# A hybrid encoder block on one Trainium2 core: decay exponents by 16 products of 128 rows, and the weighing moved off GpSimd

## The chip, the cores and the metric

The kernel runs on one core of one Trainium2 chip. Five engines work side by side, each through its own instructions in order: TensorE (PE in the profile), the vector engine (DVE), the scalar engine (ACT), GpSimd (POOL) and SyncE (SP), which here issues most of the DMAs. Matmuls write to PSUM, of which this kernel uses eight banks of 128 x 512 floats; DVE and ACT read them here, and POOL works on SBUF tiles alone. The metric is the device time of one execution in microseconds (us), the median of several runs.

## The reference

One layer with x of 256 tokens by 2048 features, all in float32. The part that the change touches is the state-space mixer: 16 heads of 64 channels in 2 groups, in two directions, over two chunks of 128 tokens.

```python
hn = rmsnorm(h, mix_norm_pre)
z, xbc, dt_raw, u = split(hn @ w_in)
xbc = silu(dwconv(xbc, conv_w, conv_b)); xs, B, C = split(xbc)
dt = softplus(dt_raw + dt_bias); a = -exp(a_log)
# in each direction, in each chunk of 128 tokens:
acum = cumsum(dt * a)
seg = acum[l] - acum[s];  decay = exp(where(s <= l, seg, -inf))
y_diag = einsum(C @ B.T, decay, xs * dt)
y_off = C @ (state of the chunk before, decayed)
y = y_fwd + y_bwd + xs * d_skip
y = rmsnorm_by_group(y * silu(z)) * norm_w
mix = concat([y, pool_mixer(u)]) @ w_out
h = h + rmsnorm(mix, mix_norm_post)
```

After it come a gated conv-MLP of width 5632 and a per-layer embedding with a gate, which the change doesn't touch.

## The kernel before

A product in float32 is made of three products in a rounded 32-bit format: each operand is split into a high part (a cast on ACT, line 150) and the rest (a subtraction on DVE, line 151). Weights come by DMA into three raw buffers, and the splits into five buffers each for high and low part, so the splits run up to five panels of 1024 columns ahead of PE.

The mixer's stage runs in this order on PE. First the columns of dt and u (tiles dtu). Then three slabs of xbc, each 512 channels: slab 2 (B and C; its conv output is bc), slab 0 (xa) and slab 1 (xb), both for xs. A slab is made by feature_major in four units of 48 matmuls, then times_rows (xr), conv (five taps: per 128 channels one ACT instruction, line 420, and four DVE instructions, line 426, 16 in all), a tanh on ACT (line 626) and a product on DVE (line 628). Then z, by token_major: eight pairs of panels with 24 matmuls each. Then the output projection (wo).

After each unit of a slab, and after each pair of z, the function aside runs the next entry of the list work. An entry is a list of jobs. The jobs are the small steps of the mixer:

- seg_prep(i), i from 0 to 7 (chunk t, quarter q of the heads): four POOL instructions multiply the step sizes (high and low part, dah and dal) by a mask, into a page ap.
- seg(i): four matmuls of 128 x 512 with the strict masks m_gt and m_lt sum these to the exponents of both directions, in one bank; ACT takes the exponential into E.
- decays: four small products and an exponential for the decay between chunks (dec).
- pool_mix and pool_map: the pooling mixer; pool_map's result leaves PSUM by ACT (cath) and DVE (catl).
- cb(g): C times B; DVE multiplies it by the masks (cbm).
- weigh(t, g): w = cbm (backward) x dt on POOL, then plus cbm (forward) x dt, eight DVE instructions, then E = E x w on DVE.
- xs_turn: transposes xs to token rows.
- far(t) and skip(t): xs x dec and xs x d_skip, both on POOL.
- mix(t, g): yo, the part from the other chunk, then yd, eight products of E with xs, added up in y.

All these jobs share two PSUM banks under the tag misc; the slabs and z use six others. Pages (13 of 128 x 2048) and mids (3 of 128 x 1024) are the SBUF buffers. The order of the instructions on each engine is not the order of the program text: a planner sorts them by the time at which they could run under a model of costs, the earlier text first among those that are ready. On the chip each engine then keeps that order, so an instruction that waits holds up all behind it on its engine. issue_after ties an instruction behind another one on the same engine.

Of the kernel before, what the change touches and what calls it, by code (L numbers as in the profile page):

```python
# [16 lines left out]
P = 128  # L17
# [4 lines left out]
H = 16  # L22
# [29 lines left out]
def build(nc, a, out):  # L52
# [5 lines left out]
    with tile.TileContext(nc) as tc, \  # L58
# [27 lines left out]
        def mm(o, lhsT, rhs, start, stop):  # L86
            nc.tensor.matmul(o, lhsT, rhs, start=start, stop=stop, skip_group_check=True)  # L87
# [24 lines left out]
        small = ep.tile([P, 80 + 512], F32, name="small")  # L112
# [18 lines left out]
        mask = small[:, 80:].rearrange("p (m f) -> p m f", m=4)  # L131
# [348 lines left out]
        with tc.issue_after(half[0]), tc.issue_after(half[1]):  # L480
            xs_ = [page(f"x{t}") for t in range(2)]
            for t in range(2):
                load(xs_[t], x[t * P:(t + 1) * P, :])
            rx = row_rstd("rx", xs_)
            m_gt, m_lt = (ep.tile([P, P], F32R, name=n) for n in ("m_gt", "m_lt"))
            nc.vector.tensor_copy(m_gt, mask[:, 2, :])
            nc.vector.tensor_copy(m_lt, mask[:, 3, :])
            aneg = ep.tile([P, 32], F32, name="aneg")
            nc.scalar.activation(aneg, alog, AF.Exp)
            nc.gpsimd.tensor_scalar(aneg, aneg, -1.0, None, op0=ALU.mult)  # L490

# [42 lines left out]
        dah = ep.tile([P, 2, 32], F32R, name="dah")  # L534
        dal = ep.tile([P, 2, 32], F32, name="dal")
        nc.vector.tensor_tensor(da, dt, aneg.unsqueeze(1).to_broadcast([P, 2, 32]), op=ALU.mult)
        nc.vector.tensor_copy(dah, da)
        nc.vector.tensor_sub(dal, da, dah.bitcast(F32))
# [13 lines left out]

        ee = [page(f"E{t}") for t in range(2)]
        steps = {}

        def seg_prep(i):
            t, q = divmod(i, 4)
            ap_ = page(f"ap{i}", F32R).rearrange("p (a h l) -> p a h l", a=4, h=4)
            for j in range(4):
                d, src = j // 2, (dah.bitcast(F32), dal)[j % 2]  # L560
                hs = slice(d * H + 4 * q, d * H + 4 * q + 4)
                nc.gpsimd.tensor_tensor(ap_[:, j], src[:, t, hs].unsqueeze(2).to_broadcast([P, 4, P]),
                                        mask[:, d, :].unsqueeze(1).to_broadcast([P, 4, P]), op=ALU.mult)
            steps[i] = ap_

        def seg(i):
            t, q = divmod(i, 4)
            sps, ap_ = misc(f"seg{i}"), steps.pop(i)
            for j in range(4):
                mm(sps, (m_gt, m_lt)[j // 2], ap_[:, j].rearrange("p h l -> p (h l)"), j == 0, j == 3)  # L570
            nc.scalar.activation(ee[t][:, q * 512:(q + 1) * 512], sps, AF.Exp)
# [59 lines left out]
        def weigh(t, g):  # L631

            w = mid(f"w{t}{g}")
            nc.gpsimd.tensor_tensor(w.rearrange("p (h l) -> p h l", h=8),
                                    cbm[:, 1, g, t, :].unsqueeze(1).to_broadcast([P, 8, P]),
                                    dt[:, t, H + 8 * g:H + 8 * g + 8].unsqueeze(2).to_broadcast([P, 8, P]),
                                    op=ALU.mult)
# [10 lines left out]
        def far(t):  # L648
            xd[t] = page(f"xd{t}")[:, :1024]
            nc.gpsimd.tensor_tensor(by_head(xd[t]), by_head(xs[:, t * 1024:(t + 1) * 1024]),  # L650
                                    dec[:, t, :].unsqueeze(2).to_broadcast([P, H, 64]), op=ALU.mult)
# [5 lines left out]
        def mix(t, g):  # L657
# [3 lines left out]
            mm(po, cbm[:, 2, g, s, :], xd[s][:, g * 512:(g + 1) * 512], True, True)  # L661
# [10 lines left out]
        def job(f, *args):  # L672
            return lambda: f(*args)
# [3 lines left out]
            [job(seg_prep, 0)],  # L677
            [job(seg_prep, 1), job(pool_mix, 0), job(pool_mix, 1)],
            [job(seg_prep, 2), job(pool_mix, 2), job(pool_mix, 3), job(decays)],
            [job(seg_prep, 3), job(seg, 0)],  # L680
# [3 lines left out]
            [job(seg_prep, 4), job(seg, 1), job(pool_map, 0), job(pool_map, 1)],  # L684
            [job(seg_prep, 5), job(seg, 2), job(cb, bc, 0), job(cb, bc, 1)],
            [job(seg_prep, 6), job(seg, 3), job(pool_map, 2), job(pool_map, 3)],
            [job(seg_prep, 7), job(seg, 4), job(weigh, 0, 0)],
# [3 lines left out]
            [job(seg, 5), job(weigh, 0, 1)],  # L691
            [job(seg, 6), job(xs_turn, xa, 0)],
            [job(seg, 7), job(weigh, 1, 0)],
            [job(weigh, 1, 1)],
# [8 lines left out]
            [],  # L703
            [job(xs_turn, xb, 1)],
# [305 lines left out]
def laid_out(a):  # L1010

    def cols(*vs):
# [11 lines left out]
            masks().transpose(1, 0, 2).reshape(P, 4 * P)], axis=1),  # L1024
# [3 lines left out]
def masks():  # L1028
    j = np.arange(P)[:, None]
    l = np.arange(P)[None, :]  # L1030
    return np.stack([j <= l, j >= l, j > l, j < l]).astype(np.float32)

# [19 lines left out]
```

## Time and profile before

| | us |
|---|---|
| median of 3 runs | 1133.08 |
| lowest and highest | 1132.37, 1133.37 |
| the profiled execution | 1134.26 |
| its span in the trace | 1132.4 |

The mixer's stage in the profiled execution, by stretches of PE's work (busy us of each engine, and TensorE's granted clock as a share of full speed):

| stretch, us | what PE works on | PE | DVE | ACT | POOL | clock |
|---|---|---|---|---|---|---|
| 53 to 82 | slab 2 | 28.36 | 21.24 | 11.51 | 17.07 | 1.00 |
| 82 to 125.3 | slab 0 | 38.36 | 36.24 | 18.23 | 26.05 | 0.92 |
| 125.3 to 152.7 | slab 1 | 26.93 | 25.61 | 13.98 | 6.74 | 1.00 |
| 152.7 to 209 | z | 56.10 | 43.66 | 23.94 | 16.21 | 1.00 |

How to read it: a row of the timeline gives the start, the length, the engine, the line, the output and inputs and, in brackets, how long the engine was idle before and what ended that. Matmuls overlap in the pipeline, so one lasts longer than the distance from its start to the next start; the distance is its cost. All matmuls are recorded under line 87, the helper mm, so they are told apart by the tile they write.

### The profile page before, as it was taken

What the parts mean: (1) busy time and instruction counts of PE and PEld (TensorE: products, weight loads), DVE (VectorE), ACT (ScalarE), POOL (GpSimd) and SP (SyncE); (2) the same over time, 40 slices, a digit from 0 to 9 for tenths busy, and PEclk for the clock granted to TensorE, in tenths of its full rate; (3) what the DMA queues carried; (4) which work ended last, traced back from release to release, by engine and by line L of the source; (5) the groups of instructions that cost most, each with busy time, mean ns of one, the idle gap of its engine ahead of it and who ended that gap; (6) DMA issues with size and microseconds to landing.
All of it is one profiled execution on the core that took longest, in us unless ns stands there. A gap on an engine that the chain in (4) does not pass through costs nothing.

```text
span 1132.4 us, 15774 instructions
## 1 busy us (share of the span) xinstructions
PE 1114.5 (98%) x5979; PEld 960.3 (85%) x5979; DVE 937.4 (83%) x1266; ACT 637.2 (56%) x868; POOL 127.3 (11%) x124
## 2 busy tenths in 40 slices
PE   9998999999999999999999999999999999999996
PEld 9997988888888888888888888888888888887875
DVE  6579797699888877878778778888899999889796
ACT  6533543465674554545545445445677777786672
POOL 0274504300101100000000000000000000001001
PEclk9998999999999999999999999999999999999998
DMA  9952347555789999998999998996969688995673
GB/s 360 344 179 81 113 128 261 205 163 184 241 302 330 328 329 312 315 295 301 348 328 313 296 316 289 330 316 213 318 194 329 222 291 304 376 306 190 231 235 109
DMA packets 145995, 300.85 MB, mean 266 GB/s; under 512 B 5504, under 2 KB 98560, under 8 KB 137856
## 3 DMA queue, kind: packets, MB, share of 16 engines
q1 hardware_dynamic: 145360, 298.44, 77.5%
q0 software_dynamic: 272, 1.05, 0.5%
q8 instruction: 47, 0.77, 0.3%
q10 hardware_dynamic: 288, 0.36, 0.1%
q14 instruction: 28, 0.23, 0.1%
HBM read 268.37 MB, written 31.46 MB: 265 GB/s over the span
## 4 chain that ended last, share of the span: by engine, by line
PE 88%; DVE 6%; DMA 2%; ACT 2%; issue 1%; POOL 1%; SPq 0%; DVEq 0%; POOLq 0%; ACTq 0%
PE va L87 22%; PE ga L87 21%; PE dna L87 12%; PE woa L87 7%; PE gt L87 5%; PE z L87 4%; PE dtu L87 4%; PE xbc L87 3%; PE dns L87 2%; DVE cv L426 2%; PE dn0s L87 1%; DMA dn138t<-dns 1%; PE dn1s L87 1%; PE ple L87 1%; DMA dtur<-w_in 1%
## 5 line engine op out<-in xcount | busy, mean ns | idle before, releaser
L87 PE MATMUL ga<-wox,ug_0h 128*128 128x512 f32 x352 | 125.6, 395 | 0.0
L87 PE MATMUL ga<-wox,ug_1h 128*128 128x512 f32 x352 | 125.1, 394 | 0.0
L87 PE MATMUL va<-wox,uv_1h 128*128 128x512 f32 x352 | 124.8, 393 | 0.0
L87 PE MATMUL va<-wox,uv_0h 128*128 128x512 f32 x352 | 124.8, 393 | 0.0
L87 PE MATMUL ga<-wox,ug_1l 128*128 128x256 f32 x352 | 99.1, 282 | 0.0
L87 PE MATMUL ga<-wox,ug_0l 128*128 128x256 f32 x352 | 99.1, 282 | 0.0
L87 PE MATMUL va<-wox,uv_1l 128*128 128x256 f32 x352 | 99.1, 281 | 0.0
L87 PE MATMUL va<-wox,uv_0l 128*128 128x256 f32 x352 | 99.1, 281 | 0.0
L87 PEld LDWEIGHTS va<-wox,uv_1h 128*128 128x128 f32 x352 | 66.1, 188 | 15.0
L87 PEld LDWEIGHTS va<-wox,uv_0h 128*128 128x128 f32 x352 | 66.1, 188 | 15.0
L87 PEld LDWEIGHTS ga<-wox,ug_0h 128*128 128x128 f32 x352 | 66.1, 188 | 14.9
L87 PEld LDWEIGHTS ga<-wox,ug_1h 128*128 128x128 f32 x352 | 66.1, 188 | 14.9
L865 POOL TENSOR_TENSOR fc<-fc,rfb 128x1024 f32<-128x1024 f32 x11 | 28.0, 2547 | 438.6 <-ACT fc L864 438.6
L87 PEld LDWEIGHTS ga<-wox,ug_0l 128*128 128x128 f32 x352 | 66.2, 188 | 0.1
L87 PEld LDWEIGHTS va<-wox,uv_1l 128*128 128x128 f32 x352 | 66.2, 188 | 0.0
L87 PEld LDWEIGHTS ga<-wox,ug_1l 128*128 128x128 f32 x352 | 66.2, 188 | 0.0
L87 PEld LDWEIGHTS va<-wox,uv_0l 128*128 128x128 f32 x352 | 66.2, 188 | 0.0
L87 PE MATMUL dna<-dn_0h,hs 128*128 128x512 f32 x160 | 50.2, 394 | 0.2 <-DVE hs L884 0.2
L87 PE MATMUL dna<-dn_1h,hs 128*128 128x512 f32 x160 | 49.9, 393 | 0.0
L233 DVE TENSOR_TENSOR dnb<-dnb 128x1024 f32<-128x1024 f32 x24 | 30.3, 1261 | 13.6 <-DMA dnb<-w_ffn_down 13.5
L883 ACT CAST hs<-hid 128x512 fp32r<-128x512 f32 x44 | 27.1, 617 | 22.9 <-PE dna L87 18.3
L884 DVE TENSOR_TENSOR hs<-hid,hs 128x512 fp32r<-128x512 f32 x44 | 30.2, 687 | 9.7 <-ACT hs L883 9.7
(1898 smaller groups left out, 3148.3 us busy)
## 6 DMA issues: line engine op xcount, KB each, us to landing
dnb<-w_ffn_down SPq DMA_DIRECT2D x24, 1024.0 KB, 10.2
dns<-dnb SPq DMA_DIRECT2D x22, 1024.0 KB, 7.6
dn0r<-w_ffn_down SPq DMA_DIRECT2D x10, 1024.0 KB, 6.3
dn1r<-w_ffn_down SPq DMA_DIRECT2D x10, 1024.0 KB, 7.0
zr<-w_in SPq DMA_DIRECT2D x8, 1024.0 KB, 5.1
dtur<-w_in SPq DMA_DIRECT2D x14, 528.0 KB, 8.9
wo0r<-w_out SPq DMA_DIRECT2D x7, 1024.0 KB, 5.8
wo1r<-w_out SPq DMA_DIRECT2D x6, 1024.0 KB, 5.5
```

The source lines that it names most:

```text
L87: nc.tensor.matmul(o, lhsT, rhs, start=start, stop=stop, skip_group_check=True)
L233: nc.vector.tensor_add(v[:, 0:2], v[:, 0:2], v[:, 1::2])
L426: nc.vector.scalar_tensor_tensor(o[:, lo:hi], i[:, lo + d:hi + d], vec(wcol + j * wstep + f), o[:, lo:hi], op0=ALU.mult, op1=ALU.add)
L865: nc.gpsimd.tensor_tensor(cv.rearrange("p (f t) -> p f t", f=4), cv.rearrange("p (f t) -> p f t", f=4), rfb.unsqueeze(1).to_broadcast([P, ...
L883: nc.scalar.copy(t[:, :512], src)
L884: nc.vector.tensor_sub(t[:, 512:], src, t[:, :512].bitcast(F32))
```

## The change

The exponents. Instead of sums over 128 tokens for each seg, seg_sums takes the running sums once for all: four products (cps, 64 rows by 128 columns for each of four pairs of chunk and direction), their high part (seg_h) and the rest (seg_c). Eight ACT instructions spread them into two pages: seg_x (the moving side) and seg_w (the weights), whose other rows hold selectors of heads, filled ahead of the first slab; the rows from 64 on are zero. seg(i) is then two products of 128 rows by 512 columns, one for each direction, in two banks: ACT copies the first to E, DVE takes the minimum of E and the second, ACT the exponential. The masks m_gt and m_lt and the whole of seg_prep are gone.

The weighing. The first half of weigh goes from one POOL instruction to eight ACT instructions; far goes from POOL to DVE. The jobs are placed anew in work: the segs from slab 2's last unit to slab 1's second, weigh(0, 0) in slab 0, weigh(0, 1) in slab 1, weigh(1, 0) and weigh(1, 1) in z's third and fourth pair. yo is tied behind the last matmul that stands before it in the text, for mix(0, 0) the last of z's sixth pair.

```diff
         def mm(o, lhsT, rhs, start, stop):
-            nc.tensor.matmul(o, lhsT, rhs, start=start, stop=stop, skip_group_check=True)
+            last["pe"] = ins(nc.tensor.matmul(o, lhsT, rhs, start=start, stop=stop, skip_group_check=True))
...
+        low, among, four = small[:64, 592:593], small[:64, 593:597], small[:64, 597:601]
...
-            m_gt, m_lt = (ep.tile([P, P], F32R, name=n) for n in ("m_gt", "m_lt"))
-            nc.vector.tensor_copy(m_gt, mask[:, 2, :])
-            nc.vector.tensor_copy(m_lt, mask[:, 3, :])
+            seg_w = page("seg_w", F32R)
+            nc.scalar.activation(seg_w[64:], xs_[0][64:], AF.Copy, scale=0.0)
+            seg_w = seg_w.rearrange("p (a q s) -> p a q s", a=4, q=4)
+            seg_x = page("seg_x", F32R)
+            nc.scalar.activation(seg_x[64:], xs_[0][64:], AF.Copy, scale=0.0)
+            seg_x = seg_x.rearrange("p (a i l) -> p a i l", a=4, i=4)
+            for a_ in range(4):
+                nc.scalar.activation(seg_w[:32, a_], four[:32].unsqueeze(2).to_broadcast([32, 4, P]), AF.Copy,
+                                     scale=-1.0)
+                nc.scalar.copy(seg_x[32:64, a_], among[32:].unsqueeze(2).to_broadcast([32, 4, P]))
...
-        dah = ep.tile([P, 2, 32], F32R, name="dah")
-        dal = ep.tile([P, 2, 32], F32, name="dal")
+        da4 = ep.tile([P, 2, 2, 4, H], F32, name="da4")
         nc.vector.tensor_tensor(da, dt, aneg.unsqueeze(1).to_broadcast([P, 2, 32]), op=ALU.mult)
-        nc.vector.tensor_copy(dah, da)
-        nc.vector.tensor_sub(dal, da, dah.bitcast(F32))
+        for d in range(2):
+            nc.vector.tensor_scalar(da4[:, :, d], da[:, :, d * H:(d + 1) * H].unsqueeze(2).to_broadcast([P, 2, 4, H]),
+                                    1.0 - 2.0 * d, None, op0=ALU.mult)
...
-        def seg_prep(i):
-            t, q = divmod(i, 4)
-            ap_ = page(f"ap{i}", F32R).rearrange("p (a h l) -> p a h l", a=4, h=4)
-            for j in range(4):
-                d, src = j // 2, (dah.bitcast(F32), dal)[j % 2]
-                hs = slice(d * H + 4 * q, d * H + 4 * q + 4)
-                nc.gpsimd.tensor_tensor(ap_[:, j], src[:, t, hs].unsqueeze(2).to_broadcast([P, 4, P]),
-                                        mask[:, d, :].unsqueeze(1).to_broadcast([P, 4, P]), op=ALU.mult)
-            steps[i] = ap_
+        def seg_sums():
+            cps = misc("cps")
+            for a_ in range(4):
+                mm(cps[:64, a_ * P:(a_ + 1) * P], da4[:, a_ // 2, a_ % 2].rearrange("p r h -> p (r h)"),
+                   mask[:, 3 * (a_ % 2), :], True, True)
+            hi, c = page("seg_h", F32R)[:64, :512], page("seg_c")[:64, :512]
+            nc.scalar.copy(hi, cps[:64, :])
+            nc.vector.scalar_tensor_tensor(c, hi.bitcast(F32), low, cps[:64, :], op0=ALU.mult, op1=ALU.add)
+            c4 = c.rearrange("p (a l) -> p a l", a=4)
+            for i in range(4):
+                nc.scalar.activation(seg_x[:32, :, i, :], c4[:32], AF.Copy, scale=among[:32, i:i + 1])
+                nc.scalar.activation(seg_w[32:64, :, i, :], c4[32:], AF.Copy, scale=four[32:, i:i + 1])
 
         def seg(i):
             t, q = divmod(i, 4)
-            sps, ap_ = misc(f"seg{i}"), steps.pop(i)
-            for j in range(4):
-                mm(sps, (m_gt, m_lt)[j // 2], ap_[:, j].rearrange("p h l -> p (h l)"), j == 0, j == 3)
-            nc.scalar.activation(ee[t][:, q * 512:(q + 1) * 512], sps, AF.Exp)
+            ps = [misc(f"seg{i}{d}") for d in range(2)]
+            for d in range(2):
+                mm(ps[d], seg_w[:, 2 * t + d, q], seg_x[:, 2 * t + d].rearrange("p i l -> p (i l)"), True, True)
+            e = ee[t][:, q * 512:(q + 1) * 512]
+            nc.scalar.copy(e, ps[0])
+            nc.vector.tensor_tensor(e, ps[1], e, op=ALU.min)
+            nc.scalar.activation(e, e, AF.Exp)
...
             w = mid(f"w{t}{g}")
-            nc.gpsimd.tensor_tensor(w.rearrange("p (h l) -> p h l", h=8),
-                                    cbm[:, 1, g, t, :].unsqueeze(1).to_broadcast([P, 8, P]),
-                                    dt[:, t, H + 8 * g:H + 8 * g + 8].unsqueeze(2).to_broadcast([P, 8, P]),
-                                    op=ALU.mult)
+            for h in range(8):
+                nc.scalar.activation(w[:, h * P:(h + 1) * P], cbm[:, 1, g, t, :], AF.Identity,
+                                     scale=dt[:, t, H + 8 * g + h:H + 8 * g + h + 1])
...
         def far(t):
             xd[t] = page(f"xd{t}")[:, :1024]
-            nc.gpsimd.tensor_tensor(by_head(xd[t]), by_head(xs[:, t * 1024:(t + 1) * 1024]),
+            nc.vector.tensor_tensor(by_head(xd[t]), by_head(xs[:, t * 1024:(t + 1) * 1024]),
                                     dec[:, t, :].unsqueeze(2).to_broadcast([P, H, 64]), op=ALU.mult)
...
-            mm(po, cbm[:, 2, g, s, :], xd[s][:, g * 512:(g + 1) * 512], True, True)
+            with tc.issue_after(last["pe"]):
+                mm(po, cbm[:, 2, g, s, :], xd[s][:, g * 512:(g + 1) * 512], True, True)
...
         work.extend([
-            [job(seg_prep, 0)],
-            [job(seg_prep, 1), job(pool_mix, 0), job(pool_mix, 1)],
-            [job(seg_prep, 2), job(pool_mix, 2), job(pool_mix, 3), job(decays)],
-            [job(seg_prep, 3), job(seg, 0)],
+            [],
+            [job(pool_mix, 0), job(pool_mix, 1)],
+            [job(pool_mix, 2), job(pool_mix, 3), job(decays), job(seg_sums)],
+            [job(seg, 0), job(seg, 1)],
         ])
         bc = xbc(2)
         work.extend([
-            [job(seg_prep, 4), job(seg, 1), job(pool_map, 0), job(pool_map, 1)],
-            [job(seg_prep, 5), job(seg, 2), job(cb, bc, 0), job(cb, bc, 1)],
-            [job(seg_prep, 6), job(seg, 3), job(pool_map, 2), job(pool_map, 3)],
-            [job(seg_prep, 7), job(seg, 4), job(weigh, 0, 0)],
+            [job(seg, 2), job(pool_map, 0), job(pool_map, 1)],
+            [job(cb, bc, 0), job(cb, bc, 1), job(seg, 3)],
+            [job(seg, 4), job(weigh, 0, 0), job(pool_map, 2)],
+            [job(seg, 5), job(pool_map, 3)],
         ])
         xa = xbc(0)
         work.extend([
-            [job(seg, 5), job(weigh, 0, 1)],
-            [job(seg, 6), job(xs_turn, xa, 0)],
-            [job(seg, 7), job(weigh, 1, 0)],
-            [job(weigh, 1, 1)],
+            [job(seg, 6)],
+            [job(seg, 7), job(weigh, 0, 1)],
+            [job(xs_turn, xa, 0)],
+            [],
         ])
...
             [],
             [],
-            [],
-            [job(xs_turn, xb, 1)],
+            [job(weigh, 1, 0)],
+            [job(xs_turn, xb, 1), job(weigh, 1, 1)],
             [job(far, 1), job(skip, 0), job(far, 0), job(skip, 1)],
             [job(mix, 0, 0)],
```

The nine further columns of small (low, among and four) come with the constants, by a new function head_rows:

```python
def head_rows():
    p = np.arange(P)[:, None]
    i = np.arange(4)[None, :]
    return np.concatenate([-((p // 16) % 2), p % 4 == i, -1.0 * (p % 16 // 4 == i)], axis=1).astype(np.float32)
```

More of the change, by code (lines that the diff above doesn't have):

```diff
@@ L111, in build @@
         vt = cp.tile([P, V_N - V_SCW], F32, name="vt")
-        small = ep.tile([P, 80 + 512], F32, name="small")
+        small = ep.tile([P, 89 + 512], F32, name="small")
         last, sums_ = {}, {}
@@ L130, in build @@
         dtb, alog, dsk = small[:, :32], small[:, 32:64], small[:, 64:80]
-        mask = small[:, 80:].rearrange("p (m f) -> p m f", m=4)
+        mask = small[:, 80:592].rearrange("p (m f) -> p m f", m=4)
+        low, among, four = small[:64, 592:593], small[:64, 593:597], small[:64, 597:601]
         def vec(i):
@@ L553, in build @@
         ee = [page(f"E{t}") for t in range(2)]
-        steps = {}
-        def seg_prep(i):
-            t, q = divmod(i, 4)
-            ap_ = page(f"ap{i}", F32R).rearrange("p (a h l) -> p a h l", a=4, h=4)
-            for j in range(4):
-                d, src = j // 2, (dah.bitcast(F32), dal)[j % 2]
-                hs = slice(d * H + 4 * q, d * H + 4 * q + 4)
-                nc.gpsimd.tensor_tensor(ap_[:, j], src[:, t, hs].unsqueeze(2).to_broadcast([P, 4, P]),
-                                        mask[:, d, :].unsqueeze(1).to_broadcast([P, 4, P]), op=ALU.mult)
-            steps[i] = ap_
+        def seg_sums():
[10 more added lines that the diff above has]
+                nc.scalar.activation(seg_w[32:64, :, i, :], c4[32:], AF.Copy, scale=four[32:, i:i + 1])
         def seg(i):
             t, q = divmod(i, 4)
-            sps, ap_ = misc(f"seg{i}"), steps.pop(i)
-            for j in range(4):
-                mm(sps, (m_gt, m_lt)[j // 2], ap_[:, j].rearrange("p h l -> p (h l)"), j == 0, j == 3)
-            nc.scalar.activation(ee[t][:, q * 512:(q + 1) * 512], sps, AF.Exp)
+            ps = [misc(f"seg{i}{d}") for d in range(2)]
[5 more added lines that the diff above has]
+            nc.scalar.activation(e, e, AF.Exp)
         cat = Panel.__new__(Panel)
@@ L1023, in laid_out @@
                             (P, 80)),
-            masks().transpose(1, 0, 2).reshape(P, 4 * P)], axis=1),
+            masks().transpose(1, 0, 2).reshape(P, 4 * P), head_rows()], axis=1),
     }
```

## The prediction

> **What bounds the kernel now.** I read the page first, for the engine that is busy most and for the chain of work that ended last.
>
> ```profile
> PE 1114.5 (98%) x5979; PEld 960.3 (85%) x5979; DVE 937.4 (83%) x1266; ACT 637.2 (56%) x868; POOL 127.3 (11%) x124
> PE 88%; DVE 6%; DMA 2%; ACT 2%; issue 1%; POOL 1%; SPq 0%; DVEq 0%; POOLq 0%; ACTq 0%
> ```
>
> PE is busy for 98% of the span. So a gain is either PE work that disappears, or one of PE's few waits. These come from the view of PE's waits, whole span:
>
> ```profile
> PE seg L87 <- DVE catl L189: 4.9, 1, 4.9
> PE dps L87 <- DVE mixt L585: 0.6, 1, 0.6
> PE xbc L87 <- DVE xb_0l L151: 0.5, 1, 0.5
> ```
>
> All three lie in the stretch that the change edits. The largest is in PE's timeline (start, length, idle before). The rows ahead of it give two prices: a pair of pool_maps takes 92.16 - 88.89 = 3.27 us, and a unit of 48 xbc matmuls 5.7, from 92.16 to 97.92:
>
> ```profile
> 88.89 3.62 PE L87 MATMUL pw<-mixt,poolw 128*128 128x256 f32 x16
> 92.16 0.47 PE L87 MATMUL xbc<-hnh,xb_0h 128*128 128x256 f32 x1
> ...
> 97.92 0.28 PE L87 MATMUL xbc<-hnh,xb_1l 128*128 128x256 f32 x1
> 103.14 1.19 PE L87 MATMUL seg<-ap,m_gt 128*128 128x512 f32 x2 [4.94 <-DVE catl L189]
> ```
>
> and the stretches after it (length, PE busy, PEld, DVE, ACT, POOL, granted clock, DMA) say what the wait costs beyond itself:
>
> ```profile
> 103.10:109.00 5.90, 5.86 (x16) 4.79 (x17) 3.50 (x7) 2.52 (x4) 1.36 (x1) 0.52 0.57 192
> 109.00:110.00 1.00, 1.00 (x11) 1.00 (x10) 0.99 (x6) 0.56 (x2) 0.53 (x1) 1.00 0.34 129
> ```
>
> After the wait the granted clock averages 0.52 for 5.9 us, then is full again: 5.9 x 0.48 = 2.83 us of work lost. What makes catl late is DVE's conv in front of it. DVE's timeline, and the durations of line 426 in the first and the second conv (min/median/max):
>
> ```profile
> 83.93 14.24 DVE L426 SCALAR_TENSOR_TENSOR cv<-xr,vt,cv 128x254 f32<-128x254 f32 x16
> 126.80 6.39 DVE L426 SCALAR_TENSOR_TENSOR cv<-xr,vt,cv 128x254 f32<-128x254 f32 x16
> L426 DVE SCALAR_TENSOR_TENSOR cv<-xr,vt,cv x16: 472/1255/1257, 83.9 to 97.7; 128x254 f32<-128x254 f32 x8, 128x255 f32<-128x255 f32 x8
> L426 DVE SCALAR_TENSOR_TENSOR cv<-xr,vt,cv x16: 470/472/474, 126.8 to 132.7; 128x254 f32<-128x254 f32 x8, 128x255 f32<-128x255 f32 x8
> ```
>
> The same 16 instructions take 14.24 us in one slab and 6.39 in the next. What differs is POOL (the stretch of the first conv, fifth busy time, and a group from 53 to 210 us):
>
> ```profile
> 84.00:97.00 13.00, 13.00 (x95) 12.41 (x94) 13.00 (x15) 3.58 (x5) 12.30 (x12) 1.00 0.12 44
> L562 POOL TENSOR_TENSOR ap<-dal,small 128x512 fp32r<-128x512 f32 x16 | 22.4, 1400 | 0.0
> ```
>
> POOL is busy for 12.30 of 13.00 us, with seg_prep, and DVE's instruction takes 1255 ns; in the second conv, in the pause after seg_prep, it takes 472.
>
> **What the change removes.** *The decay matmuls.* Each seg now has two 512-column products instead of four:
>
> ```profile
> 81.34 0.62 PE L87 MATMUL seg<-ap,m_gt 128*128 128x512 f32 x2
> 81.80 0.62 PE L87 MATMUL seg<-ap,m_lt 128*128 128x512 f32 x2
> 71.97 2.02 PE L87 MATMUL mx<-pmat,u 128*128 128x136 f32 x16
> 73.74 0.37 PE L87 MATMUL xbc<-hnh,xb_0h 128*128 128x256 f32 x1
> ```
>
> Two start 0.46 after the other two, so a product is 0.23 us and 16 fewer save 3.68. PE also gains four fp32 products of 128 columns (cps). The mx group is two pool_mix jobs, 8 fp32 products, in 16 records of 136 columns; they take 73.74 - 71.97 = 1.77; the new ones are 8 records, so 0.88. Bounds: 0.4 if half of that overlaps, 1.1 if PE must wait for a weight load.
>
> *seg_prep on POOL* goes altogether. The first conv then takes 6.39 instead of 14.24, 7.85 us less in front of th, cv and catl. Nothing on DVE then is late for PE: the wait of 4.94 and its 2.83 go, and with the contention the two small waits (0.6 for a mixt copy behind a stretched split, 0.5 for a split), together 1.1.
>
> **What it adds.** The prices:
>
> ```profile
> 202.06 0.69 DVE L670 TENSOR_TENSOR y<-y,yd 128x512 f32<-128x512 f32 x1 [1.56 <-PE yd L87]
> L639 DVE SCALAR_TENSOR_TENSOR w<-cbm,dt,w 128x128 f32<-128x128 f32 x32 | 12.1, 444 | 1.8 <-POOL w L634 1.8
> L643 DVE TENSOR_TENSOR E<-E,w 128x1024 f32<-128x1024 f32 x3 | 3.6, 1215 | 0.0
> L409 DVE TENSOR_TENSOR xr<-xbc,rxb 128x512 f32<-128x512 f32 x3 | 2.0, 678 | 0.0
> L189 DVE SCALAR_TENSOR_TENSOR catl<-pw,vt,cath 128x256 fp32r<-128x256 f32 x8 | 3.7, 480 | 1.5 <-ACT cath L188 1.3
> L571 ACT ACTIVATE E<-seg 128x512 f32<-128x512 f32 x8 | 4.7, 593 | 0.5 <-PE seg L87 0.5
> L420 ACT ACTIVATE cv<-xr,vt 128x256 f32<-128x256 f32 x8 | 4.4, 593 | 0.0
> L611 ACT ACTIVATE cbm<-cb 128x128 f32<-128x128 f32 x4 | 1.1, 278 | 3.4 <-DVE cbm L609 3.3
> 82.00:125.30 43.30, 38.36 (x250) 35.65 (x249) 36.24 (x53) 18.23 (x30) 26.05 (x22) 0.92 0.29 98
> 125.30:152.70 27.40, 26.93 (x213) 25.92 (x212) 25.61 (x50) 13.98 (x19) 6.74 (x4) 1.00 0.31 100
> ```
>
> Each seg gets an ACT copy (0.59) and a DVE min (0.69, same form as y plus yd) before its exp: 4.7 us on ACT, 5.5 on DVE in all. weigh's POOL pass becomes eight ACT instructions, each between 0.28 (128 wide, from PSUM) and 0.59 (256 wide, two vectors); I take 0.35, 2.8 per call, as the width is that of the cheaper row. Does this fit? In the two slabs DVE was busy 36.24 + 25.61 = 61.85. Minus 7.85 (conv), minus the two of four weighs that move into z (2 x (12.1/4 + 1.2) = 8.5), plus 5.5: 51. PE's own time there is 70.7 - 8.2 (stall and clock) - 3.2 (segs 1 to 7) = 59. ACT: 18.23 + 13.98 + 4.7 + 5.6, 42 of 59. Neither sets the pace.
>
> ACT's one-time work for seg_w and seg_x (two clears 2048 wide, eight copies 512 wide) lies before the first slab:
>
> ```profile
> 36.34 1.92 ACT L391 ACTIVATE rxj<-x 128x2048 f32<-128x2048 f32 x1
> 40.00:60.00 20.00, 20.00 (x143) 20.00 (x142) 11.71 (x22) 10.60 (x15) 2.64 (x5) 1.00 0.84 288
> 51.65 0.56 ACT L514 ACTIVATE u<-dtu,rx0r 128x352 f32<-128x352 f32 x1 [6.52 <-PE dtu L87]
> ```
>
> 2 x 1.92 + 8 x 0.59 = 8.6 us, against 6.52 idle just before L514 and 9.4 from 40 to 60 (ACT busy 10.60): covered. If only the 6.52 served, 2.1 would fall on u's evacuation, which frees banks for the first slab: bounds 0 to 2.1, taken 0. seg_sums' chain (hi copy, c, eight more 512-wide ACT copies, about 6 us) runs under unit 3 of slab 2, 48 matmuls or 5.7 us, and the splits are several panels ahead: taken 0, up to 1.
>
> far on DVE (two ops of 1024, 1.2 each as the E product) and the late weighs sit under z. The tie moves nothing; the chain of waits already has yo behind six pairs (96 + 48 matmuls, 24 to a pair):
>
> ```profile
> 152.89 22.26 PE z L87 x96
> 176.02 11.10 PE z L87 x48
> 187.12 0.86 PE yo L87 x2
> ```
>
> *The new wait.* A seg takes both misc banks and gives the second back only after the min, which in slab 0's first unit is queued on DVE behind the conv. PE's arrival at pool_map 1, counted from the start of slab 0: segs 0 and 1, 48 matmuls, seg 2, pool_map 0 (half of 3.27) = 0.9 + 5.7 + 0.5 + 1.6 = 8.7. DVE, from the same point: last matmul's length 0.3 + xr 1.36 + two mins 1.38 + conv 6.39 + min 0.69 = 10.1. So 1.4 us if the matmuls stay in the order of the job list, 0 if others are put between, as the transposes show (xt, xbc, xt):
>
> ```profile
> 138.56 0.60 PE L617 MATMUL xt<-ident,cv 128*128 128x128 f32 x4
> 138.92 0.36 PE L87 MATMUL xbc<-hnh,xb_0h 128*128 128x256 f32 x1
> ...
> 139.41 0.65 PE L617 MATMUL xt<-ident,cv 128*128 128x128 f32 x4
> ```
>
> I take 0.7. Behind it wait catl, then cb; but th, its product (1.2 each, as the E product) and four catl (0.48 each) end by 10.1 + 2.4 + 1.9 = 14.4 on DVE, and PE comes to cb at 8.7 + 1.6 + 5.7 = 16.
>
> **Sum.** 3.68 - 0.88 + 4.94 + 2.83 + 1.1 - 0.7 = 10.97 us. The profiled execution took 1134.26 (span 1132.4), so 1123.3 in its terms; it stands 1.18 above the median of the runs, so 1133.08 - 10.97 = **1122.1**.
>
> **Rivals.** *One long wait stays.* If two splits (1024 wide, 1.2 each as the E product) are put ahead of the conv on DVE, PE's 1.4 us becomes 3.8, and as after the 4.94 the clock may drop, 2.8 more. 11.67 (the sum without its 0.7) less 6.6 leaves 5.1: 1128. For it: the catl wait had just this shape. Against: in the second slab the conv ran at 6.39 and PE waited 0.5.
>
> *Every hand-over of the two banks is unfilled* (slower). Then PE idles for copy and min, 0.59 + 0.69 = 1.28, at each of eight segs: 10.3, leaving 1.4 of gain. It decides from the first drop of the clock (2.8), which turns this to a loss of 1.4; with two drops the loss is 4.3, 1137.4. Against: the xt rows show such gaps filled, and the idles of 0.6 and 0.5 cost only themselves. [...]
>
> *The contention stays (the change doesn't do what it says).* If the first conv is slow for another reason, stall and clock loss stay and the mins add to it: 3.68 - 0.88 - 1.4 = 1.4, 1131.7. The 1255 against 472 ns speaks against it.
>
> **How the numbers follow.** A change under 0.2% (2.3 us) can't be told from none. The forecast has 0.75, with its own range 1119.8 (no new wait 1121.4, cps at its lower bound 0.5 less, a run's scatter) to 1125; one long wait 0.12; contention 0.03; the slower rival 0.08; 0.02 is left for a loss I don't see. Faster 0.75 + 0.12 = 0.87, same 0.03, slower 0.10. The range goes to 1130.5 to hold the 1128 case with its scatter.
>
> **What would show it.** Right: the first conv near 6.4 us; no PE idle over 2 us between 53 and 200; clock 1.00 in every stretch there; seg steps 0.46; z beginning near 141 instead of 152.7. Wrong: PE idle at a seg or pool_map with a min (or seg_x) as releaser; a clock of 0.50; the first conv still near 14; ACT late at 51 us. The forecast fails if the waits on the two banks add up to more than 4 us.

## The result, and the profile after

The median is 1123.84 us (four runs, 1123.31 to 1123.89) against 1132.94 for the kernel before (four runs, 1132.37 to 1133.37): a ratio of 0.9918, interval 0.9907 to 0.9930, a gain of 9.1 us. The profiled execution after took 1123.86 us (span 1122.1), so it stands at its median, where the one before, 1134.26, stood 1.2 above.

From the page of the changed kernel, the busy times and the chain of work that ended last:

```profile
PE 1109.2 (99%) x5971; PEld 957.8 (85%) x5971; DVE 925.4 (82%) x1275; ACT 664.3 (59%) x927; POOL 76.0 (7%) x86
PE 95%; ACT 2%; DVE 1%; issue 1%; POOL 1%; DMA 0%; POOLq 0%; DVEq 0%; ACTq 0%
```

PE's share of the chain rose from 88 to 95%, DVE's fell from 6 to 1. POOL lost 51 us of work and ACT gained 27. The view of PE's waits, from 50 to 200 us, where the first line was 4.9 before, has one line above 0.2:

```profile
PE seg L87 <- ACT seg_x L579: 0.7, 1, 0.7
```

Busy time by stretch (length, PE, PEld, DVE, ACT, POOL, granted clock, DMA share, GB/s):

```profile
82.00:115.00 33.00, 32.28 (x231) 30.37 (x230) 27.48 (x54) 26.26 (x47) 0.00 (x0) 1.00 0.37 115
115.00:140.00 25.00, 24.99 (x198) 24.33 (x197) 23.59 (x42) 17.40 (x30) 0.00 (x0) 1.00 0.44 151
140.00:200.00 60.00, 59.80 (x303) 49.13 (x302) 45.84 (x67) 29.89 (x48) 16.87 (x10) 1.00 0.60 209
```

The clock is full in all three, and POOL has nothing left in the two slabs. The first conv, in DVE's timeline, cut in two by a min:

```profile
87.64 1.77 DVE L428 SCALAR_TENSOR_TENSOR cv<-xr,vt,cv 128x254 f32<-128x254 f32 x4
89.33 0.69 DVE L589 TENSOR_TENSOR E<-seg,E 128x512 f32<-128x512 f32 x1
89.93 4.82 DVE L428 SCALAR_TENSOR_TENSOR cv<-xr,vt,cv 128x255 f32<-128x255 f32 x12
94.66 0.69 DVE L589 TENSOR_TENSOR E<-seg,E 128x512 f32<-128x512 f32 x1
```

It takes 1.77 + 4.82 = 6.59 us instead of 14.24. PE's timeline has the one wait left in this stretch, a seg of the third slab made (slab 1), and the beginning of z:

```profile
85.68 0.73 PE L87 MATMUL seg<-seg_x,seg_w 128*128 128x512 f32 x2 [0.69 <-ACT seg_x L579]
...
130.37 0.63 PE L87 MATMUL seg<-seg_x,seg_w 128*128 128x512 f32 x2
130.83 0.28 PE L87 MATMUL xbc<-hnh,xb_0h 128*128 128x256 f32 x1
...
143.10 0.63 PE L87 MATMUL z<-z_0h,hnh 128*128 128x512 f32 x2
```

A seg is 130.83 - 130.37 = 0.46 us for PE, half of before, and z begins at 143.10 instead of 152.72.

### The profile page after: what moved, and what is told of

It is laid out like the page before. It is cut to its first block, busy times and chain, and to the rows that moved or that the text cites. A ratio compares the mean times of both kernels' runs of the same rounds, so it can differ in the third digit from the quotient of the medians.

```text
span 1122.1 us, 15775 instructions
## 1 busy us (share of the span) xinstructions
PE 1109.2 (99%) x5971; PEld 957.8 (85%) x5971; DVE 925.4 (82%) x1275; ACT 664.3 (59%) x927; POOL 76.0 (7%) x86
## 4 chain that ended last, share of the span: by engine, by line
PE 95%; ACT 2%; DVE 1%; issue 1%; POOL 1%; DMA 0%; POOLq 0%; DVEq 0%; ACTq 0%
PE va L87 22%; PE ga L87 21%; PE dna L87 14%; PE woa L87 7%; PE xbc L87 6%; PE gt L87 5%; PE dtu L87 4%; PE z L87 4%; PE dns L87 3%; PE dn0s L87 1%; PE dn1s L87 1%; PE ple L87 1%; PE pw L87 1%; PE yd L87 0%; PE gts L87 0%
```

## The experiments

Ratios are against the kernel before, timed beside each on the same chip. "After" means the changed kernel. Whole times also hold what differs at the beginning and the end of an execution, so the table gives, for each profiled execution, the time, the start of PE's first matmul of slab 2, and what PE takes from there to its first matmul of z, the stretch that the change edits (all in us, from the traces).

| kernel | profiled execution | slab 2 begins | slab 2 to z |
|---|---|---|---|
| before | 1134.26 | 52.91 | 99.81 |
| before, profiled again | 1132.27 | 52.93 | 98.54 |
| before, weigh and far moved alone | 1131.98 | 52.54 | 98.69 |
| before, seg_prep once | 1124.81 | 52.75 | 91.26 |
| after | 1123.86 | 53.39 | 89.71 |
| after, POOL work put back | 1135.15 | 52.81 | 100.80 |
| after, weigh and far back on POOL | 1123.88 | 52.54 | 89.69 |
| after, weighs at their old places | 1131.26 | 54.57 | 89.83 |
| after, yo untied | 1123.06 | 52.56 | 89.73 |
| after, seg products twice | 1126.68 | 52.83 | 93.10 |
| after, 64 rows | 1126.00 | 52.69 | 92.44 |
| after, spreads on POOL | 1123.14 | 52.77 | 89.52 |
| after, spreads on POOL, maps in pairs | 1123.10 | 52.80 | 89.39 |

Slab 2 begins from 0.9 us earlier to 1.2 later in the kernels made from after than in after itself, though nearly all of their edits lie behind that point. So a difference of about 1 us between whole times is no effect by itself.

**The POOL work put back into the changed kernel.** The 32 products of the old seg_prep run again on POOL at their old places in the work lists; nothing reads them.

```diff
+        def busy(i):
+            t, q = divmod(i, 4)
+            ap_ = page(f"ap{i}", F32R).rearrange("p (a h l) -> p a h l", a=4, h=4)
+            for j in range(4):
+                d = j // 2
+                hs = slice(d * H + 4 * q, d * H + 4 * q + 4)
+                nc.gpsimd.tensor_tensor(ap_[:, j], da[:, t, hs].unsqueeze(2).to_broadcast([P, 4, P]),
+                                        mask[:, d, :].unsqueeze(1).to_broadcast([P, 4, P]), op=ALU.mult)
```

> The changed kernel, with the 32 POOL products of the old seg_prep added back at their old places; nothing reads them. Theory (POOL's work stretches DVE's conv, and that made PE wait): the 16 conv instructions of the first slab take about 14 us again instead of 6.6, a PE wait of 2 us or more comes back near the pool_map or cb products, and the time rises by 4 to 9 us over the changed kernel (1128 to 1133). Rival (the gain came from the other order of the jobs and from fewer matmuls): the conv may stretch, but PE does not wait; the time stays within 1.5 us of 1123.8.

Measured: 1134.88 us (1133.91 to 1135.4), ratio 1.0017 (1.0008 to 1.0026). The whole gain is gone, and 2 us more, somewhat beyond what the theory expected. The two longest of PE's waits in this kernel (a third, of 1.0 us at dps, is for a mixt copy, as before the change):

```profile
PE pw L87 <- DVE E L598: 2.6, 1, 2.6
PE seg L87 <- DVE E L598: 2.5, 1, 2.5
```

DVE's timeline:

```profile
89.61 4.68 DVE L428 SCALAR_TENSOR_TENSOR cv<-xr,vt,cv 128x254 f32<-128x254 f32 x4
94.22 0.68 DVE L598 TENSOR_TENSOR E<-seg,E 128x512 f32<-128x512 f32 x1
94.82 8.91 DVE L428 SCALAR_TENSOR_TENSOR cv<-xr,vt,cv 128x255 f32<-128x255 f32 x12
103.65 0.68 DVE L598 TENSOR_TENSOR E<-seg,E 128x512 f32<-128x512 f32 x1
```

and the stretches around the first of the two waits (columns as above):

```profile
92.00:95.00 3.00, 0.53 (x5) 0.20 (x3) 3.00 (x4) 1.06 (x3) 3.00 (x3) 0.99 0.00 0
95.00:98.00 3.00, 3.00 (x13) 2.91 (x14) 3.00 (x4) 2.93 (x4) 2.92 (x4) 0.50 0.00 0
```

The conv is back at 4.68 + 8.91 = 13.6 us with no other edit than POOL's work, so the contention is shown (what the two engines share is in no trace). And the prediction's worry about the two misc banks becomes real here: two mins stand in DVE's queue behind stretched conv pieces, PE waits for each bank, and after 2.5 us of idling the clock is at 0.50. It falls to 0.50 again soon after the second wait, for 3.41 us each time. Between this kernel and after lie 11.0 us that POOL's products alone cost.

**seg_prep once, in the kernel before.** Only the first call forms its products; the other seven calls reuse them, so their exponents are left out of the computation. PE has the same matmuls as before.

```diff
+            if i:
+                steps[i] = steps[0]
+                return
...
-            sps, ap_ = misc(f"seg{i}"), steps.pop(i)
+            sps, ap_ = misc(f"seg{i}"), steps[i]
```

> The kernel before, with seg_prep's four POOL products made once, for i = 0, and read by all eight segs, so that all 32 seg matmuls stay and POOL is idle during the conv; the exponents of the other quarters and of the second chunk are left out. Theory (POOL's work is the cause of the 4.9 us wait and the 2.8 us of half clock): conv 6.4 us, that wait and the 0.6 and 0.5 waits gone, 7.5 to 9 us faster than before: 1124 to 1125.5. Rival (the wait comes from the order of jobs and the two banks): the wait stays above 2 us and the time above 1129.

Measured: 1125.01 us (1124.76 to 1125.12), ratio 0.9931 (0.9918 to 0.9943), 7.7 us below the 1132.73 beside it. DVE's first conv:

```profile
82.79 6.39 DVE L426 SCALAR_TENSOR_TENSOR cv<-xr,vt,cv 128x254 f32<-128x254 f32 x16
```

The 4.94 us wait for catl is gone, and so is the one of 0.6 at dps; the wait for a split of xbc stays, at 0.4, which the theory did not expect. So most of the change's gain is had by taking the work off POOL; the new matrix products, the mins and the moved jobs together bring the other 1.4 (1.55 in the table, 91.26 - 89.71).

**The kernel before, profiled again.** No edit.

> The kernel before, unchanged, for a second profile. Question: which of the terms taken from the first profile (wait 4.94, clock loss 2.83, 1.1 of small waits) is larger there than in another execution, since that execution took 1.2 us more than the median. Theory (the share of half clock depends on when the pause falls): wait 4.9 to 5.0 again, clock loss between 1.5 and 2.8. Rival: the waits themselves are shorter.

Measured: 1132.27 us (one run). PE's timeline:

```profile
103.15 1.19 PE L87 MATMUL seg<-ap,m_gt 128*128 128x512 f32 x2 [4.94 <-DVE catl L189]
```

and the stretch behind it:

```profile
103.00:109.00 6.00, 5.85 (x27) 5.15 (x28) 4.62 (x12) 3.28 (x7) 1.66 (x1) 0.74 0.55 189
```

The wait is the same to the hundredth. The lowered clock now takes 6.0 x 0.26 = 1.56 us from this stretch, of which 0.07 falls before PE begins at 103.15, so it costs 1.5 us; in the execution on which the prediction rests it cost 2.83. The table agrees: 99.81 - 98.54 = 1.27 us lie between the two executions from slab 2 to z.

**weigh on ACT and far on DVE, alone, in the kernel before.** (Two of the moves, at the old places, with seg_prep as it was.)

```diff
-            nc.gpsimd.tensor_tensor(w.rearrange("p (h l) -> p h l", h=8),
-                                    cbm[:, 1, g, t, :].unsqueeze(1).to_broadcast([P, 8, P]),
-                                    dt[:, t, H + 8 * g:H + 8 * g + 8].unsqueeze(2).to_broadcast([P, 8, P]),
-                                    op=ALU.mult)
+            for h in range(8):
+                nc.scalar.activation(w[:, h * P:(h + 1) * P], cbm[:, 1, g, t, :], AF.Identity,
+                                     scale=dt[:, t, H + 8 * g + h:H + 8 * g + h + 1])
...
-            nc.gpsimd.tensor_tensor(by_head(xd[t]), by_head(xs[:, t * 1024:(t + 1) * 1024]),
+            nc.vector.tensor_tensor(by_head(xd[t]), by_head(xs[:, t * 1024:(t + 1) * 1024]),
```

> The kernel before, with only the first half of weigh moved to ACT and far to DVE, at the old places. Theory (this part brings nothing by itself; the 4.9 us wait is made by seg_prep): within 1.5 us of the kernel before, 1131.5 to 1134, the wait at seg and the half clock still there. Rival (a good part of the gain is this): 3 us or more faster than before.

Measured: 1132.52 us (11 runs, 1131.78 to 1133.21), ratio 0.9997 (0.9988 to 1.0005): nothing. From PE's waits, and the stretch behind the wait:

```profile
PE seg L87 <- DVE catl L189: 5.0, 1, 5.0
```

```profile
103.10:109.00 5.90, 5.90 (x25) 4.99 (x25) 4.12 (x10) 3.42 (x10) 0.00 (x0) 0.67 0.55 184
```

The wait stays as it was. The clock's loss is a third value: 5.9 x 0.33 = 1.95 us here, and 0.17 more because PE's seg begins at 102.76, 0.34 us ahead of the stretch, with the clock at 0.50 already. That makes 2.1 us.

**weigh and far back on POOL, in the changed kernel.** The reverse edit.

> The changed kernel, with the first half of weigh and with far back on POOL, the jobs at their new places. Theory (these moves cost and bring PE nothing, because they lie beside it): within 1 us of the changed kernel, though DVE's instructions beside them stretch. Rival (the move off POOL is a part of the gain): 2 us or more slower.

Measured: 1123.89 us (1123.83 to 1124.42), ratio 0.9923 (0.9910 to 0.9935). From slab 2 to z it is 89.69 us against 89.71. The engine on which these two jobs run does not matter, in either kernel.

**The four weighs at their old places, in the changed kernel.**

```diff
-            [job(seg, 4), job(weigh, 0, 0), job(pool_map, 2)],
-            [job(seg, 5), job(pool_map, 3)],
+            [job(seg, 4), job(pool_map, 2)],
+            [job(seg, 5), job(pool_map, 3), job(weigh, 0, 0)],
...
-            [job(seg, 6)],
-            [job(seg, 7), job(weigh, 0, 1)],
-            [job(xs_turn, xa, 0)],
-            [],
+            [job(seg, 6), job(weigh, 0, 1)],
+            [job(seg, 7)],
+            [job(xs_turn, xa, 0), job(weigh, 1, 0)],
+            [job(weigh, 1, 1)],
...
-            [job(weigh, 1, 0)],
-            [job(xs_turn, xb, 1), job(weigh, 1, 1)],
+            [],
+            [job(xs_turn, xb, 1)],
```

> The changed kernel with the four weighs at the places they had before (slab 0's last unit, slab 1's first, third and last). Theory (DVE then has about 32 us of work for the 28 us of slab 1, but its splits are several panels ahead, and z takes up the rest): 0 to 1 us slower. Rival A (DVE falls behind, PE waits for splits in slab 1 or at the start of z): 1.5 us or more slower. Rival B: faster by 0.5 us or more.

Measured: 1128.48 us (1127.5 to 1131.26), ratio 0.9966 (0.9954 to 0.9979): 4.6 us slower than after. Beside the 0.7 at seg_x PE has one more wait, in z:

```profile
PE z L87 <- DVE z_0l L153: 3.2, 1, 3.2
```

DVE's timeline there:

```profile
146.59 6.49 DVE L428 SCALAR_TENSOR_TENSOR cv<-xr,vt,cv 128x254 f32<-128x254 f32 x16 [0.17 <-ACT cv L422]
153.00 1.22 DVE L153 TENSOR_TENSOR z_0l<-zr,z_0h 128x1024 fp32r<-128x1024 f32 x1
```

With all four weighs ahead of z, DVE has no room before the third conv, and the split that z needs stands behind it. In after the same split, the second z_0l, starts at 137.75. This trace is of the slowest of the five executions, 1131.26 us, 7.4 above after: 1.2 are a later beginning of slab 2, 3.2 are the wait, and from its end at 154.27 to 159.9 the clock is at 0.50, which costs 2.8. By the medians the places are worth 4.6 us, though the engines are worth none.

**yo untied.**

```diff
-            with tc.issue_after(last["pe"]):
-                mm(po, cbm[:, 2, g, s, :], xd[s][:, g * 512:(g + 1) * 512], True, True)
+            mm(po, cbm[:, 2, g, s, :], xd[s][:, g * 512:(g + 1) * 512], True, True)
```

> The changed kernel without the tie of yo. Theory (the planner already put yo behind z's sixth pair before, so the tie moves nothing): within 0.5 us of the changed kernel, yo at the same place among z's pairs. Rival (without it, since far is now done earlier, yo is planned earlier and PE waits for it or its bank): 1 us or more slower, with a PE wait at yo or yd.

Measured: 1124.19 us (1123.06 to 1125.53), ratio 0.9924 (0.9912 to 0.9936); yo again stands behind the sixth pair of z, 34.1 us after z's first matmul as in after. The tie moves nothing. Two of the five executions took 1125.4 and 1125.5 us; the trace is of the fastest, and what held those two up is not shown.

**Each seg product twice, in the changed kernel.**

```diff
-                mm(ps[d], seg_w[:, 2 * t + d, q], seg_x[:, 2 * t + d].rearrange("p i l -> p (i l)"), True, True)
+                for _ in range(2):
+                    mm(ps[d], seg_w[:, 2 * t + d, q], seg_x[:, 2 * t + d].rearrange("p i l -> p (i l)"), True, True)
```

> The changed kernel, with each of the 16 seg products issued twice into the same bank. Theory (a product of 128 x 512 costs PE its 0.23 us, since nothing hides it): 16 x 0.23 = 3.7 us more, 1127.5. Rival (PE has slack in the two slabs, because DVE and ACT set the pace there): under 1.5 us more.

Measured: 1126.56 us (1126.38 to 1126.86), ratio 0.9945 (0.9933 to 0.9957), 2.7 above after where 3.7 was expected. PE's timeline:

```profile
132.73 1.08 PE L87 MATMUL seg<-seg_x,seg_w 128*128 128x512 f32 x4
133.65 0.28 PE L87 MATMUL xbc<-hnh,xb_0h 128*128 128x256 f32 x1
```

Four products take 0.92 us, 0.23 each: the price per product holds. From slab 2 to z PE takes 93.10 - 89.71 = 3.4 us more, so nearly the whole price is paid there. Most of the missing microsecond is that slab 2 began 0.56 us earlier in this execution than in after's.

**Sixty-four rows instead of 128.** The upper 64 rows of seg_w and seg_x are zero; here the products take the lower 64 alone, and the two clears go.

```diff
-                mm(ps[d], seg_w[:, 2 * t + d, q], seg_x[:, 2 * t + d].rearrange("p i l -> p (i l)"), True, True)
+                mm(ps[d], seg_w[:64, 2 * t + d, q], seg_x[:64, 2 * t + d].rearrange("p i l -> p (i l)"), True, True)
...
-            nc.scalar.activation(seg_w[64:], xs_[0][64:], AF.Copy, scale=0.0)
```

> The changed kernel with seg's products over 64 rows instead of 128, without the zero rows and the two ACT clears of 1.9 us. Theory (a product costs by its columns, and the clears lie under ACT's idle time): within 0.7 us of the changed kernel. Rival A (the clears delay u and the first slab): 0.5 us or more faster, slab 2 beginning at 52.9 instead of 53.4. Rival B (64 rows cost PE more, or break its flow): 1 us or more slower.

Measured: 1126.0 us (1125.91 to 1127.02), ratio 0.9941 (0.9929 to 0.9954), 2.2 slower than after for less work. PE's timeline around one seg:

```profile
131.88 0.28 PE L87 MATMUL xbc<-hnh,xb_1l 128*128 128x256 f32 x1
132.09 0.73 PE L87 MATMUL seg<-seg_x,seg_w 64*128 64x512 f32 x2
...
132.98 0.28 PE L87 MATMUL xbc<-hnl,xb_0h 128*128 128x256 f32 x1
```

From the xbc matmul ahead to the second one behind are 1.10 us; two xbc matmuls (0.12 each) and two products (0.23 each) make 0.70, so a visit costs 0.40 more, where in after it costs nothing at the same place (130.37 to 130.83 above). The four other visits of two products that have no wait before them take 1.09 or 1.10 us as well. What PE does in the 0.40 no row shows. Ten visits at 0.40 would be 4.0 us, and the stretch from slab 2 to z grew by 2.7. By PE's timelines the four pool_maps came out 0.7 cheaper here, and after's segs lose some 0.4 themselves, which leaves 2.9. Rival A's sign came too: slab 2 began at 52.69, 0.37 behind the transposes as before the change, but the gain of that is lost in the visits.

**The seg_w spreads on POOL, in the changed kernel.** This goes for the one wait left. Four of the eight copies that spread c move from ACT to POOL, which is idle there.

```diff
-                nc.scalar.activation(seg_w[32:64, :, i, :], c4[32:], AF.Copy, scale=four[32:, i:i + 1])
+                nc.gpsimd.tensor_scalar(seg_w[32:64, :, i, :], c4[32:], four[32:, i:i + 1], None, op0=ALU.mult)
```

> The changed kernel with the four seg_w spreads of seg_sums on POOL, beside the four seg_x spreads on ACT. Theory (PE's one wait of 0.7 us at the first seg comes from the chain of eight ACT instructions of 0.72): the wait goes, and the time falls by 0.5 to 1 us. Rival (POOL needs longer than ACT for them, or stretches xr on DVE): the wait stays or grows, time the same or up to 1 us slower.

Measured: 1123.19 us (1123.14 to 1123.32), ratio 0.9915 (0.9901 to 0.9928), 0.65 below after, as expected. In PE's timeline the first seg carries no wait:

```profile
82.60 0.70 PE L87 MATMUL seg<-seg_x,seg_w 128*128 128x512 f32 x2
```

But the stretch from slab 2 to z is only 0.2 us shorter than after's (89.52 against 89.71). The wait went, but most of its 0.7 was given back: summed over PE's timelines, the ends of the segs' visits cost 0.4 more than in after and those of the maps 0.1. The rest of the 0.65 is, in the profiled executions, an earlier beginning of slab 2, ahead of what was edited. So the wait's cause is shown, but the time came out as expected mostly by luck.

**The same, with pool_maps in pairs.** Maps 0 and 1, and 2 and 3, stand together ahead of a seg, as before the change.

```diff
-            [job(seg, 2), job(pool_map, 0), job(pool_map, 1)],
+            [job(pool_map, 0), job(pool_map, 1), job(seg, 2)],
...
-            [job(seg, 4), job(weigh, 0, 0), job(pool_map, 2)],
-            [job(seg, 5), job(pool_map, 3)],
+            [job(pool_map, 2), job(pool_map, 3), job(seg, 4), job(weigh, 0, 0)],
+            [job(seg, 5)],
```

> The changed kernel with seg_w spread on POOL (as in h3), and pool_maps 0 and 1 as well as 2 and 3 put one behind the other ahead of a seg, so that PE goes from 32-bit-rounded to plain float32 products and back twice instead of four times. Theory (each such visit costs PE about 0.35 us at its two ends, as a pool_map in the changed kernel begins 0.29 and its successor's second matmul 0.30 after the one before instead of 0.12): 0.5 to 1 us faster than with h3 alone, 1122.2 to 1122.7. Rival (the two maps take both banks and hold the seg and cb behind DVE): a PE wait at seg or cb, not faster.

Measured: 1123.28 us (1123.1 to 1123.63), ratio 0.9917 (0.9903 to 0.9930): no faster. PE's timeline, a pair of maps and then one product of seg 4:

```profile
106.90 0.28 PE L87 MATMUL xbc<-hnh,xb_1l 128*128 128x256 f32 x1
107.02 3.62 PE L87 MATMUL pw<-mixt,poolw 128*128 128x256 f32 x16
110.28 0.47 PE L87 MATMUL xbc<-hnh,xb_0h 128*128 128x256 f32 x1
110.59 0.28 PE L87 MATMUL xbc<-hnl,xb_0h 128*128 128x256 f32 x1
...
110.83 0.28 PE L87 MATMUL xbc<-hnh,xb_0h 128*128 128x256 f32 x1
111.02 0.50 PE L87 MATMUL seg<-seg_x,seg_w 128*128 128x512 f32 x1
111.36 0.28 PE L87 MATMUL xbc<-hnl,xb_0h 128*128 128x256 f32 x1
```

The maps did get cheaper: entered at a unit's beginning, a pair costs its 3.26 us and 0.19 on the way out. But the segs, now behind the maps, fall into the middle of a unit and are split into single products, and this one takes 111.36 - 110.83 = 0.53 from xbc to xbc instead of 0.12 + 0.23 = 0.35. What the maps save (0.8 us, summed over PE's timelines) the segs give back for the most part (0.7). The step was also smaller than the theory had it: in the kernel with only the spreads moved, maps 0 and 1 stand together on PE already, so the maps go from three visits to two, not from four.

## Why the prediction held, and where it was off

The forecast was 1122.1 us, a gain of 11.0; it was 9.1. The mechanism was right in each link: POOL's products stretched the conv (the two POOL experiments), the late conv made catl late, and PE lost time to the wait and then to the clock. The signs it named came out: the conv at 6.59 (near 6.4), no idle of PE above 0.7, a clock of 1.00, steps of 0.46, z at 143.1 (141 was named).

*The half clock was mis-sized.* It was entered at 2.83 us, from one execution. After the same wait the two other executions with it lost 1.5 and 2.1. The prediction took this term from a profile 1.2 us above the median, but subtracted the sum from the median, and so counted that execution's bad luck as a gain. With 1.5 the sum is 9.6. The run with seg_prep once agrees: 0.4 of the small waits stayed there, 4.94 + 1.5 + 0.7 is 7.1, and from slab 2 to z it is 98.54 - 91.26 = 7.3 us shorter than the second profile (7.7 by the medians). Read in pieces of 0.1 us, the granted clock stayed at 0.50 for 6.83 us in the first profile, with weigh and far moved alone, and with the weighs at their old places, and for 3.41 us in the second profile and after each of the two waits with the POOL work put back. That is once or twice the same 3.41 us, and the loss is half of that part of it in which PE has work: at 0.50 two seg products took 0.99 us in the first profile, from 103.14 to 104.13, instead of 0.46. Nor does it begin at one point of the wait: in the first profile at 101.9 us, 3.7 us after PE fell idle, and in the second, an estimate from the loss of 1.56 us between 103 and 109, 4.5 us after. What sets its beginning, and whether it is 3.41 us or twice that, no run shows.

*The wait at pool_map 1*, taken at 0.7, did not come. After's PE timeline between the two maps:

```profile
93.73 0.47 PE L87 MATMUL xbc<-hnh,xb_0h 128*128 128x256 f32 x1
...
95.47 0.29 PE L87 MATMUL xbc<-hnl,xb_1h 128*128 128x256 f32 x1
95.59 1.24 PE L87 MATMUL pw<-mixt,poolw 128*128 128x256 f32 x5
```

PE did xbc matmuls from 93.73 until the min that began at 94.66 had freed the bank, so the wait came out at the lower end of 0 to 1.4.

*The chain of seg_sums*, taken at 0 with up to 1, ended in the 0.69 us of the wait at the first seg. ACT's timeline:

```profile
79.55 1.05 ACT L152 CAST xb_1h<-xb0r 128x1024 fp32r<-128x1024 f32 x1 [0.91 <-PE xbc L87]
80.50 0.72 ACT L579 ACTIVATE seg_x<-seg_c,small 32x512 fp32r<-32x512 f32 x1
...
84.90 0.72 ACT L579 ACTIVATE seg_x<-seg_c,small 32x512 fp32r<-32x512 f32 x1
```

The spreads take 0.72 us each, not the 0.59 of the row it was priced by, and begin behind a cast; the last but one ends as PE starts its seg. Half of them on POOL removed the wait, though not its whole price, as said. The same chain also held up DVE, which idled 3.79 us ahead of its first min (87.02 us, released by the copy to E on ACT); so the conv began at 87.64 us instead of 83.93, without any wait of PE for it.

*Visits of PE.* One term was a little small, and one was not seen. After's PE timeline at cps and at a single pool_map:

```profile
76.93 1.09 PE L87 MATMUL cps<-small,da 128*64 128x128 f32 x8
77.95 0.38 PE L87 MATMUL xbc<-hnh,xb_0h 128*128 128x256 f32 x1
...
109.22 0.28 PE L87 MATMUL xbc<-hnh,xb_0l 128*128 128x256 f32 x1
109.53 1.99 PE L87 MATMUL pw<-mixt,poolw 128*128 128x256 f32 x8
111.17 0.47 PE L87 MATMUL xbc<-hnh,xb_0h 128*128 128x256 f32 x1
111.48 0.28 PE L87 MATMUL xbc<-hnl,xb_0h 128*128 128x256 f32 x1
```

cps costs 77.95 - 76.93 = 1.02 where 0.88 was entered, and 0.1 beyond an xbc step at each end, 0.3 more than entered in all. The single map takes 1.64, and 0.19 more than an xbc step both before and after it; a pair that begins with a unit pays 0.19 once. That the change splits two pairs into four visits was not priced at all. Worked out in the same way for this visit, it costs 2 x (1.64 + 0.38) - (3.26 + 0.19) = 0.6 us per pair, 1.2 in all at most, since not each of the four pays the full price. Added up with their ends in PE's timelines, the four maps take 7.64 us after and 6.90 before: 0.7.

*Covered work.* ACT's one-time work before the first slab was taken at 0, with 2.1 as the bound. Before, the first xbc followed the rxbp transposes after 0.36 us (PE's timeline of the kernel before); after, it does so after 0.57, as soon as the first evacuation of u is done (ACT's and PE's timelines):

```profile
52.55 0.61 PE L87 MATMUL rxbp<-ident,rxbw 128*128 128x128 f32 x4
52.91 0.36 PE L87 MATMUL xbc<-hnh,xb_0h 128*128 128x256 f32 x1
```

```profile
52.79 0.54 ACT L524 ACTIVATE u<-dtu,rx0r 128x352 f32<-128x352 f32 x1
```

```profile
52.82 0.61 PE L87 MATMUL rxbp<-ident,rxbw 128*128 128x128 f32 x4
53.39 0.38 PE L87 MATMUL xbc<-hnh,xb_0h 128*128 128x256 f32 x1
```

That is 0.2 us. So 9.6, with the 0.7 at seg_x in place of the one at pool_map 1, less 0.3 for cps, 0.2 here and 0.7 for the maps, makes 8.4. The executions of 1132.27 and 1123.86 us differ by 8.4 too, which is closer than the terms are known: the transposes already began 0.25 us later in after, a difference that stands in PE's rows at 13 us, long before the change's instructions. From slab 2 to z the two differ by 98.54 - 89.71 = 8.8. The medians differ by 9.1: the second profile of the kernel before is of one of its fastest executions, and the loss to the clock differs from one execution to the next.

*The moves.* "Lie beside other work" was right for far, weigh's engine and the tie: each is worth nothing alone. The places of the weighs are another matter. The prediction had them in its sum for DVE, 8.5 us that move into z and leave 51 of 59, and put no price on them; with the 8.5 back the sum would have been 59.5 of 59, and the chip lost 4.6 us at the one split that z had to wait for. So "neither sets the pace" held because of the move, not beside it.

*The rivals.* One long wait did not stay: no split came between the xr and the end of the conv on DVE, and the longest wait of the stretch was 0.7. The rival with every hand-over of the two banks unfilled did not come true: PE was filled and its clock stayed at 1.00 through all ten visits of seg. It was no empty threat: with POOL's work left in, this kernel has two such hand-overs unfilled (2.6 and 2.5 us), a drop of the clock to 0.50 for 3.41 us after each, and is slower than before (a ratio of 1.0017). Contention that stays was ruled out by the conv's 6.59.

## What to carry to other kernels

An engine that sits idle 89% of the span can still set the end: look at what the same instruction of another engine costs with and without it (14.24 against 6.39 us here), and try the removal alone before a rewrite, for it may be most of the gain. Work out a stall's cost in clock from more than one execution, and compare variants over the stretch that was edited, not by whole times alone: a gain of 0.65 us was mostly an earlier beginning. And count visits as well as products: on a busy PE, entering and leaving in the middle of a unit added 0.38 us to a map of 1.64.

## What was not expected of the hardware

Products of 64 rows among products of 128 cost 0.40 us per visit, so zero rows were cheaper than fewer rows, by 2.2 us in all. After one and the same wait of 4.94 to 5.0 us the lowered clock cost 2.8, 1.5 and 2.1 us in three executions; it stayed at 0.50 for 6.83, 3.41 and 6.83 us, and what of that fell into the wait (1.2 us in the first) cost nothing. In the kernel with POOL's work back, a stretch at 0.50 followed 2.5 us of idling. A visit in the middle of an xbc unit cost PE up to 0.38 us beyond its products (a single pool_map), at a unit's beginning 0 (a seg) to 0.19 (a pair of maps); why some visits in the middle cost the lower figure was not found.
